# A gradient along rows: a strip of 512 columns of the last tile goes through DMAs of its own

## The chip, the cores and the metric

The kernel runs on one core of a Trainium2 chip. The metric is device time in microseconds (us): the time of one execution on the core, and over several runs the median. A profile of one execution, taken by the hardware profiler, goes with it; its span, from the first to the last instruction of the program, is a little shorter than the time of a run.

The engines that matter here are DVE (VectorE), POOL (GpSimd), SP (SyncE, which only issues DMAs here) and the core's 16 DMA engines, which move data between the chip's memory (HBM) and the core's memory (SBUF, 128 partitions).

## The reference

```python
def setup_inputs():
    return {
        "x": np.random.randn(8192, 8192).astype(np.float32),
    }

def reference(x: np.ndarray) -> np.ndarray:
    return np.gradient(x, axis=1)
```

Along each row, an inner element is `(x[j+1] - x[j-1]) / 2`; the first is `x[1] - x[0]` and the last `x[8191] - x[8190]`. All is float32. 268.4 MB are read and as many are written, and each row can be worked on by itself.

## The kernel before

**Tiles.** The 8192 rows are cut into `nsets` = 32 tiles of 256 rows. A tile lies in SBUF with two whole rows (`R` = 2) in each of the 128 partitions, so that a partition holds 65,536 B, in one piece in HBM as well. There are `NB` = 3 buffers (`slots`); tile i uses slot i % 3. A slot is 64 elements (`SH`) longer than a tile: the load writes from element 64 on, and the result is written from element 0 on, so it is made in place, running behind its input.

**One tile.** Six steps follow each other, each with the wait that it needs:

- L60, `load`: SP issues the load of the tile into its slot. From tile 3 on it waits for the store of the tile that had the slot before.
- L70: POOL computes the two end columns of each row (4 elements a partition) into `ends`, once the load has landed.
- L76: DVE computes all inner elements in one pass over 16,382 elements a partition, after L70. At the seam between the two rows and at their ends this pass leaves values that are no result.
- L87: the end columns are copied from `ends` over those places, by POOL for tiles with i % 5 of 1 or 3 (the last two excepted), else by DVE.
- L89: SP issues the store of the tile, after L87.
- After each third tile SP issues the next three loads.

**Order.** The program is in a fixed order (`tc.manual_schedule()`): each engine runs its instructions in the order in which the code names them. On SP that is load 0, 1, 2, store 0, 1, 2, load 3, 4, 5, store 3, 4, 5, and so on to load 30, load 31, store 30, store 31, since the last group has two tiles. All DMAs of the kernel stand in SP's one queue, and each tile DMA is spread over all 16 DMA engines: 128 pieces of 65,536 B, eight for each. POOL issues no DMA. `chain` keeps only the dependencies that it is given, and the order within a slot.

**What the change touches.** The loads at the start, `load` for the last tile, what follows tile 0 and tile 29 in the main loop, and the last store. In the order of SP, the new DMAs of the first half stand between load 0 and load 1 and between store 0 and store 1; on POOL the new DMAs of the second half stand between the end columns of tile 29 and those of tile 30; on DVE the new work stands behind L87 of tile 0 and behind L87 of tile 29.

Of the kernel before, what the change touches and what calls it, by code (L numbers as in the profile page):

```python
# [1 line left out]

# [4 lines left out]


@with_exitstack
def kernel(  # L10
    ctx: ExitStack,
    tc: tile.TileContext,
    x: bass.AP,
    out: bass.AP,
):

    nc = tc.nc
    P = nc.NUM_PARTITIONS
    n, m = x.shape
    R = 2
    NB = 3  # L30
    SH = 64
    W = R * m
    nsets = n // (P * R)
    f32 = x.dtype

    x_sets = x.rearrange("(s p t) m -> s p (t m)", p=P, t=R)
    out_sets = out.rearrange("(s p t) m -> s p (t m)", p=P, t=R)

    pool = ctx.enter_context(tc.tile_pool(name="pool", bufs=1))
    slots = [pool.tile([P, SH + W], f32, name=f"slot{k}", tag=f"slot{k}") for k in range(NB)]  # L40
    ends = pool.tile([P, nsets, R, 2], f32, name="ends", tag="ends")
    loads, stores = [], [None] * nsets
    in_front = {}

    def chain(i, ins, *needed):

        group, engine = f"slot{i % NB}", ins.ins.engine
        keep = [o.ins for o in needed]  # L50
        if in_front.get(engine, (None,))[0] == group:
            keep.append(in_front[engine][1])
        tc.declare_no_dep(ins.ins, group=group, keep=keep, reason="implied by the needed step")
        tc.add_to_no_dep_group(group, ins.ins)
        in_front[engine] = group, ins.ins
        return ins

    def load(i):
        b = slots[i % NB]
        ins = nc.sync.dma_start(out=b[:, SH : SH + W], in_=x_sets[i])  # L60
        loads.append(chain(i, ins, *([stores[i - NB]] if i >= NB else [])))

    with tc.manual_schedule():
        for i in range(NB):
            load(i)
        for i in range(nsets):
            b = slots[i % NB]
            xin = b[:, SH : SH + W].rearrange("p (t m) -> p t m", m=m)

            ins = nc.gpsimd.tensor_sub(  # L70
                out=ends[:, i, :, :],
                in0=xin[:, :, 1 : m : m - 2],
                in1=xin[:, :, 0 : m - 1 : m - 2],
            )
            at = [chain(i, ins, loads[i])]
            ins = nc.vector._custom_dve(  # L76
                dve_ops.TENSOR_TENSOR_REDUCE_SUB_MAX,
                out=b[:, 1 : W - 1],
                in0=b[:, SH + 2 : SH + W],
                in1=b[:, SH : SH + W - 2],  # L80
                s0=0.0,
                s1=0.5,
            )
            halved = chain(i, ins, *at)
            res = b[:, 0:W].rearrange("p (t m) -> p t m", m=m)
            placer = nc.gpsimd if i % 5 in (1, 3) and i < nsets - 2 else nc.vector
            ins = placer.tensor_copy(out=res[:, :, 0 : m : m - 1], in_=ends[:, i, :, :])  # L87
            placed = chain(i, ins, halved)
            ins = nc.sync.dma_start(out=out_sets[i], in_=b[:, 0:W])  # L89
            stores[i] = chain(i, ins, placed)  # L90
            if i % NB == NB - 1:
                for k in range(i + 1, min(i + 1 + NB, nsets)):
                    load(k)


# [1 line left out]
_INS = ['x']  # L97
_OUTS = [((8192, 8192), 'float32')]


# [23 lines left out]
```

## Time and profile before

| | |
|---|---|
| time, median of 3 runs | 1248.46 us (1248.35 to 1248.61) |
| span of the profiled execution | 1245.7 us |
| DVE's main pass (L76) | 32 x 17.22 us = 551.2 us |
| POOL waiting for loads to land (L70) | 989.6 us |
| data moved | 536.88 MB, 431 GB/s over the span |
| one tile load, from issue to landing (median) | 58.0 us |
| one tile store, from issue to landing (median) | 40.4 us |

The profiled execution is one execution; its own time isn't listed beside its span, and the median of the runs is 2.8 us above that span. Times inside the profile count from the start of the span. In the lines of the page, DMA digits are the busy share of the DMA engines in each of 40 slices, in tenths; `q1` is SP's DMA queue and `q14` the queue that brings instructions. In a timeline a line has the start, the duration, the engine, the source line and the operation, and in brackets the idle time before it with what ended it; `SPq` is the issue of a DMA by SP, and with `x2` it spans from the first issue to the end of the second.

### The profile page before, as it was taken

What the parts mean: (1) busy time and instruction counts of PE and PEld (TensorE: products, weight loads), DVE (VectorE), ACT (ScalarE), POOL (GpSimd) and SP (SyncE); (2) the same over time, 40 slices, a digit from 0 to 9 for tenths busy, and PEclk for the clock granted to TensorE, in tenths of its full rate; (3) what the DMA queues carried; (4) which work ended last, traced back from release to release, by engine and by line L of the source; (5) the groups of instructions that cost most, each with busy time, mean ns of one, the idle gap of its engine ahead of it and who ended that gap; (6) DMA issues with size and microseconds to landing.
All of it is one profiled execution on the core that took longest, in us unless ns stands there. A gap on an engine that the chain in (4) does not pass through costs nothing.

```text
span 1245.7 us, 237 instructions
## 1 busy us (share of the span) xinstructions
DVE 554.6 (45%) x52; POOL 8.8 (1%) x48
## 2 busy tenths in 40 slices
DVE  2850583069009702850582079009603840591083
POOL 0000000000000000000000000000000000000000
DMA  9999999999999999999999999999999999999999
GB/s 404 438 436 423 427 431 438 438 438 436 436 427 431 425 438 436 425 434 436 429 434 436 434 436 434 436 434 438 419 436 436 434 438 438 431 434 429 429 410 404
DMA packets 9217, 536.88 MB, mean 431 GB/s; under 512 B 1024, under 2 KB 1024, under 8 KB 1024
## 3 DMA queue, kind: packets, MB, share of 16 engines
q1 hardware_dynamic: 9216, 536.88, 99.8%
q14 instruction: 1, 0.01, 0.0%
HBM read 268.44 MB, written 268.44 MB: 431 GB/s over the span
## 4 chain that ended last, share of the span: by engine, by line
another core or an unknown queue 74%; DVE 18%; DMA 3%; issue 2%; POOL 1%; SPq 0%; POOLq 0%
DVE slot L76 18%; DMA slot<-in_x_dram 3%; POOL ends L70 0%; POOL slot L87 0%; SPq L60 0%; POOLq L119 0%; DVE slot L87 0%
## 5 line engine op out<-in xcount | busy, mean ns | idle before, releaser
L76 DVE CUSTOM_DVE_ANT_0 slot<-slot 128x16382 f32<-128x16382 f32 x32 | 551.2, 17224 | 668.7 <-POOL ends L70 668.7
L70 POOL TENSOR_TENSOR ends<-slot 128x4 f32<-128x4 f32 x32 | 6.3, 198 | 989.6 <-DMA slot<-in_x_dram 989.6
L87 POOL COPY slot<-ends 128x4 f32<-128x4 f32 x12 | 2.3, 190 | 207.9 <-DVE slot L76 207.9
L87 DVE COPY slot<-ends 128x4 f32<-128x4 f32 x20 | 3.4, 172 | 0.7
L108 POOL MEMSET const-bfloat16-1.0<- 128x1 bf16 x1 | 0.1, 101 | 0.0
L108 POOL MEMSET const-uint8-127<- 128x1 uint8 x1 | 0.1, 101 | 0.0
L108 POOL MEMSET const-float32-0.0<- 128x1 f32 x1 | 0.1, 98 | 0.2 <-issue 0.2
L108 POOL MEMSET const-float32-1.0<- 128x1 f32 x1 | 0.1, 98 | 0.0
## 6 DMA issues: line engine op xcount, KB each, us to landing
slot<-in_x_dram SPq DMA_DIRECT2D x32, 58.0
out_dram<-slot SPq DMA_DIRECT2D x32, 40.4
```

Of the source, the lines that this page charges most:

```text
L70: ins = nc.gpsimd.tensor_sub(out=ends[:, i, :, :], in0=xin[:, :, 1 : m : m - 2], in1=xin[:, :, 0 : m - 1 : m - 2],)
L76: ins = nc.vector._custom_dve(dve_ops.TENSOR_TENSOR_REDUCE_SUB_MAX, out=b[:, 1 : W - 1], in0=b[:, SH + 2 : SH + W], in1=b[:, SH : SH + W - 2],
L87: ins = placer.tensor_copy(out=res[:, :, 0 : m : m - 1], in_=ends[:, i, :, :])
L108: nc = _bacc.Bacc("TRN2", target_bir_lowering=False, num_devices=1)
```

## The change

The last tile (rows 7936 to 8191) is made 512 columns (`D`) narrower. Its load brings columns 0 to 7680 (one more than is stored, for the difference at the edge) and its store writes columns 0 to 7679, each as two pieces a partition instead of one. DVE's pass over the tile is not made shorter; what it computes to the right of the cut is not stored.

The 512 last columns of those 256 rows become two strips of 128 rows, in a new tile `strip` of 32 partitions with four rows each, for each half. Every strip DMA has eight rows of pieces (`G` = 8), one row of four in each of eight partitions, and four such DMAs carry a half.

- First half: SP issues its four loads behind load 0. After tile 0 DVE computes it (`strip_finish`: end column, difference, times 0.5, copy of the end column), and SP issues its four stores behind store 0.
- Second half: after tile 29, DVE clears a small tile `turn`; then POOL issues the four loads, each behind a small load of 8 x 64 B into `turn` (`other_engines`). DVE computes the half before it goes on to tile 30, and POOL issues the four stores, each again behind a small load into `turn`. The data in `turn` is used by nothing.

```diff
+    D = 512
+    G = 8
+    C = D + 1
+    last = nsets - 1
+    base = last * P * R
+
+    def tiles_of(dram):
+        return dram.rearrange("(s p t) m -> s p (t m)", p=P, t=R)
+
+    def cut_of(dram, width):
+        return dram.rearrange("(s p t) m -> s p t m", p=P, t=R)[last][:, :, 0:width]
+
+    def strip_of(dram, first, per, width):
+        rows = dram[base + first : base + first + G * per, m - width : m]
+        return rows.rearrange("(g q) w -> g q w", q=per)
+
+    x_sets, out_sets = tiles_of(x), tiles_of(out)
...
+    strip = pool.tile([P, 4, C], f32, name="strip", tag="strip")
+    tips = pool.tile([P, 4, 1], f32, name="tips", tag="tips")
+    turn = pool.tile([G, 8, 16], f32, name="turn", tag="turn")
+    queues = nc.sync, nc.gpsimd
...
     def load(i):
-        b = slots[i % NB]
-        ins = nc.sync.dma_start(out=b[:, SH : SH + W], in_=x_sets[i])
+        b = slots[i % NB][:, SH : SH + W]
+        of = x_sets[i]
+        if i == last:
+            b = b.rearrange("p (t m) -> p t m", m=m)[:, :, 0 : m - D + 1]
+            of = cut_of(x, m - D + 1)
+        ins = nc.sync.dma_start(out=b, in_=of)
         loads.append(chain(i, ins, *([stores[i - NB]] if i >= NB else [])))
 
+    def strip_part(dram, half, k, width):
+        rows = strip_of(dram, half * G * 16, 16, width)[:, 4 * k : 4 * k + 4, :]
+        first = half * P // 2 + k
+        return rows, strip[first : first + 4 * (G - 1) + 1 : 4, :, 0:width]
+
+    def other_engines(half, k):
+        if half:
+            nc.gpsimd.dma_start(out=turn[:, k, :], in_=x[0:G, 0:16])
+
+    def strip_loads(half):
+        for k in range(4):
+            rows, cells = strip_part(x, half, k, C)
+            other_engines(half, k)
+            queues[half].dma_start(out=cells, in_=rows)
+
+    def strip_finish(half):
+        part = slice(half * P // 2, half * P // 2 + 4 * G)
+        cells, tip = strip[part], tips[part]
+        inner = cells[:, :, 0 : C - 2]
+        nc.vector.tensor_sub(out=tip, in0=cells[:, :, C - 1 : C], in1=cells[:, :, C - 2 : C - 1])
+        nc.vector.tensor_sub(out=inner, in0=cells[:, :, 2:C], in1=inner)
+        nc.vector.tensor_scalar_mul(inner, inner, 0.5)
+        nc.vector.tensor_copy(out=cells[:, :, C - 2 : C - 1], in_=tip)
+        for k in range(4):
+            rows, cells = strip_part(out, half, k, D)
+            other_engines(half, 4 + k)
+            queues[half].dma_start(out=rows, in_=cells)
+
     with tc.manual_schedule():
-        for i in range(NB):
-            load(i)
+        load(0)
+        strip_loads(0)
+        load(1)
+        load(2)
         for i in range(nsets):
             b = slots[i % NB]
+            width = m - D if i == last else m
...
-            ins = nc.sync.dma_start(out=out_sets[i], in_=b[:, 0:W])
+            to, of = out_sets[i], b[:, 0:W]
+            if i == last:
+                to, of = cut_of(out, width), res[:, :, 0:width]
+            ins = nc.sync.dma_start(out=to, in_=of)
             stores[i] = chain(i, ins, placed)
+            if i == 0:
+                strip_finish(0)
+            if i == last - 2:
+                nc.vector.memset(turn, 0.0)
+                strip_loads(1)
+                strip_finish(1)
```

More of the change, by code (lines that the diff above doesn't have):

```diff
@@ L34 @@
     f32 = x.dtype
-    x_sets = x.rearrange("(s p t) m -> s p (t m)", p=P, t=R)
-    out_sets = out.rearrange("(s p t) m -> s p (t m)", p=P, t=R)
+    D = 512
[11 more added lines that the diff above has]
+    x_sets, out_sets = tiles_of(x), tiles_of(out)
     pool = ctx.enter_context(tc.tile_pool(name="pool", bufs=1))
```

## The prediction

> **What bounds the kernel now.** I read the busy shares and DMA queues first, then windows and the timeline at the end, then the DMA packet records.
>
> From the page (engines, slices, queues):
>
> ```profile
> span 1245.7 us, 237 instructions
> DVE 554.6 (45%) x52; POOL 8.8 (1%) x48
> ...
> DMA  9999999999999999999999999999999999999999
> ...
> q1 hardware_dynamic: 9216, 536.88, 99.8%
> q14 instruction: 1, 0.01, 0.0%
> ```
>
> The 16 DMA engines are full: SP's queue holds packets for 99.8% of 16 engines' span. The packet records say the same: each engine moves 512 packets of 65,536 B; the usual one takes 2.418 us, so 1238.0 us. The rest is 4.2 us in slower packets (mostly the first of a store after a load), 0.6 us in 4-byte completion packets (9 ns each), 1.7 us before the first packet and 1.2 us after the last: 1245.7 in all (neighbouring packets overlap by some 4 ns, 2 us an engine, about as much as the hole below). The change moves the same bytes, so the most that it could win is a few us.
>
> Windows (stretch, length, DVE, POOL, granted PE clock, DMA share, GB/s):
>
> ```profile
> 1128.00:1187.00 59.00, 0.00 (x0) 0.07 (x1) 1.00 1.01 438
> 1203.00:1205.50 2.50, 1.56 (x2) 0.00 (x0) 1.00 0.49 210
> 1205.50:1225.00 19.50, 17.40 (x2) 0.20 (x1) 1.00 1.05 454
> ```
>
> There is one hole: half the DMA time from 1203.0 to 1205.5. The timeline tells why:
>
> ```profile
> 1127.16 0.17 DVE L87 COPY slot<-ends 128x4 f32<-128x4 f32 x1
> 1127.36 0.33 SPq L89 DMA_DIRECT2D out_dram<-slot  x1
> 1128.95 19.64 SPq L60 DMA_DIRECT2D slot<-in_x_dram  x2
> 1186.93 0.20 POOL L70 TENSOR_TENSOR ends<-slot 128x4 f32<-128x4 f32 x1 [77.07 <-DMA slot<-in_x_dram]
> 1187.17 17.22 DVE L76 CUSTOM_DVE_ANT_0 slot<-slot 128x16382 f32<-128x16382 f32 x1 [59.84 <-POOL ends L70]
> 1204.42 0.17 DVE L87 COPY slot<-ends 128x4 f32<-128x4 f32 x1
> 1204.62 19.69 SPq L89 DMA_DIRECT2D out_dram<-slot  x2
> 1206.28 0.20 POOL L70 TENSOR_TENSOR ends<-slot 128x4 f32<-128x4 f32 x1 [19.14 <-DMA slot<-in_x_dram]
> 1206.51 17.23 DVE L76 CUSTOM_DVE_ANT_0 slot<-slot 128x16382 f32<-128x16382 f32 x1 [1.91 <-POOL ends L70]
> 1223.77 0.17 DVE L87 COPY slot<-ends 128x4 f32<-128x4 f32 x1
> ```
>
> Tile 30 lands at 1186.9. Its arithmetic and its store's start take 18.5 us (the store is issued at 1204.62, its first packets start at 1205.47). Meanwhile the load of tile 31 (8 x 2.418 = 19.3 us an engine) ends on the engines between 1202.8 and 1205.8, by following each engine's packets. So 15 engines wait 0.1 to 2.8 us (mean 1.6) and one, the slowest, does not. From there the two last stores run without a hole to 1244.5. The end is therefore set by: tile 30's landing on the slowest engine, 18.5 us, and two stores.
>
> **The change, part by part.**
>
> *Smaller last tile.* Per engine, eight packets of 2.418 us become sixteen half ones. By rate (65,536 B in 2.418 us, 27.1 B/ns) 30,720 B take 1.134 us, so 16 take 18.14 instead of 19.34, less 0.07 for eight more packets at 9 ns: 1.13 us less for the load and for the store. The store's 1.13 counts in full. The load's does not: the store of tile 30 waits for arithmetic, 18.5 us after tile 30's landing, and the shorter load (18.2) only makes the hole longer, on the slowest engine too. DVE works the full width as before; that chain stays.
>
> *SP's strips.* Four loads between the loads of tiles 0 and 1, four stores behind store 0: eight issues of 0.34 us, hidden behind 19.3 us packets already queued (without that cover 2.7 us). On eight engines each brings 16 pieces of 2,052 B in and 16 of 2,048 B out. A piece is 0.076 us by rate; the fixed part is between 9 ns (a completion packet) and 268 ns (the extra explained below), so 16 pieces cost 1.4 to 5.5 us. They stand in one ring with their neighbours, as the completion packets do: I take 1.4 in and 1.4 out.
>
> *Early DVE work.* Two passes over 4x511 elements at 1.051 ns (17,224 ns for 16,382) and two copies of 0.17: 4.65 us between tile 0 (done at 40.4) and tile 1 (landing at 42.0, with the strips 43.4). Tile 1 starts near 45.3, 3 us late, and its store, queued on SP behind the four strip stores, is issued near 62.8 instead of 59.8; it is needed when store 0 ends, at 81.8. Store 2 moves by less than 1 us. Cost nothing; without that cover 3 us.
>
> *Pool's strips.* The memset of `turn` follows tile 29's copy on DVE, so Pool issues four decoys and four loads from about 1127.5. A Pool issue isn't in this trace: between SP's 0.34 us and the 1.0 us from SP's first issue to its first packet; I take 0.7. Eight are 5.6 us in Pool's idle 77 us. SP's queue has stores 28 and 29 and loads 30 and 31 standing until 1205, so each Pool packet takes its turn. One row shows a turn: the instruction packet (8,192 B) at 997.7 us was served on one engine between the third and fourth 64 KB packets of one DMA, took 0.30 us, and the next packet took 2.686 instead of 2.418. So a turn comes after at most 2.42 us, and a foreign packet costs 0 to 0.27 us beyond its bytes. A strip DMA brings 4 pieces, 8,208 B, to an engine, about that packet's size: as one packet it costs 0.57 us and four cost 2.3. Completion packets and decoys (64 B an engine) lie between 9 ns and 0.27 us; four at the middle, 0.14, are 0.5 us. So loads add 2.8 us on the late eight engines. The early eight get four decoys at the full 0.27 (they change direction inside a store stream, where slow packets are found) and four completions, 1.6 us.
>
> *When they land.* Four to 24 turns (one for each DMA, or one for each piece, completion and decoy) are 10 to 58 us. I take 8, two a DMA, 19.4 us, since the 8 KB packet went in one: landed near 1149, DVE done near 1154, Pool's stores and decoys (4.9 us) issued by 1159 and through their 8 turns near 1179. Behind them on Pool stands tile 30's `ends` at 1186.9, and behind that DVE's main pass: 77 us of idle cover both; if it is gone each us late is a us at the end.
>
> On turns the row and the notes differ. The Trainium skill (DMA: Bandwidth & Descriptors, "Queues, rings and completion order") says that an engine drains a whole packet, typically 9 to 17 descriptors, before it turns to another queue. A turn would then be a whole tile DMA of 19.3 us, eight turns 155 us; the strips would land only as SP's queue runs dry near 1206, and DVE, Pool and two stores after that would end near 1281 in the median's terms. The packet served after three of eight speaks against it, and I go by the row.
>
> *The sum.* Before tile 30's landing the early eight gain 1.4 + 1.4 + 1.6, and 1.6 more for the store phase: 6.0 us. The late eight gain 2.8 + 2.8 = 5.6. Whichever half holds the slowest engine, the landing moves by 5.6 to 6.0, and I take 5.5, for the slow packets that overlap with it. Less 1.13 for the last store: +4.4 us. The profiled execution becomes 1250.1; the median of the runs stands 2.8 us above its span (1248.46 against 1245.7), which I keep: **1252.9 us**.
>
> Ends: by bytes alone, with Pool's stores in the hole, landing moves 1.2 to 2.4, so +0.1 to +1.3; with 268 ns a piece on SP's strips too, about +13.
>
> **The rivals.**
>
> *Strips cost only their bytes (not slower).* Place: the hole ahead of store 30. Price: if a foreign packet adds nothing (completion packets add 9 ns), the early eight gain 2.4 to 2.8 us and the late eight 1.2 to 1.4 each way, Pool's stores filling the hole. Landing moves 2.4, less 1.13: +1.3, 1249.8 us. It becomes a gain only from the point where the landing moves by less than 1.13, that is if the slowest engine is so far behind the eight that get most; the best is then -1.1, 1247.3. For it: completion packets cost 9 ns, and direction changes from store to load cost nothing in most groups. Against: the one foreign packet cost 0.57 us, not 0.30.
>
> *A new wait at tile 30.* If each piece takes a turn (24 x 2.42 = 58 us), strips land at 1186.5, DVE ends at 1191.2, Pool's seven issues at 1196.1, `ends` and the main pass at 1213.7, and store 30 starts at 1214.8 instead of 1205.5. +9.3 - 1.13 = +8.2: 1256.7 us; with issues of 1.0 us (+2.1) and two turns more (+4.8), 1263.6. It decides from 20 turns on: (1186.9 - 4.65 - 4.9 - 1128.4)/2.42. For it: the records show 64 KB pieces as packets of their own. Against: 8 KB went in one.
>
> *The change doesn't do what it says.* If the decoys don't steer, Pool's strips fall on the early eight: 2.8 + 2 x (2.3 + 0.5) = 8.4, less 1.13: +7.3, 1255.8 us. No row shows on which engines a Pool DMA of eight rows falls. The same page of the skill ("Why a DMA increments its semaphore by 16 and not by 1") says that it takes consecutive engines from a cursor that goes round, which the decoys rely on; no run here shows it.
>
> **How the numbers follow.** Forecast 0.45, bytes alone 0.34, new wait 0.14, no steering 0.07. About 0.2% (2.5 us) is what a measurement of this kernel tells from no change, so 1246.0 to 1251.0 is "same". Of bytes alone 0.03 is faster and 0.31 same; of the forecast, if foreign packets cost a third of the row, 0.05 is same. Faster 0.03, same 0.36, slower 0.61. The range cuts the gaining end of bytes alone (about 0.12) and the far end of the new wait (0.06): 1248.6 to 1262; the forecast's own range is 1250.5 to 1256.
>
> **What would show it.** Right: a DMA queue of Pool with strip packets spread over the stretch from 1128 on, 64 KB packets after them longer than 2.418 us; tile 30's `ends` some 5 us later than 1186.9; a longer hole ahead of store 30, about 1 us shorter from there to the end. Wrong: tile 30's `ends` waiting for POOL or DVE instead of the load (new wait); tile 30 landing at most 2.4 us later (bytes alone); eight engines far behind the other eight at the last load (no steering).

## The result and the profile after

Over 21 runs each on the same chips, the changed kernel takes 1249.48 us (1248.06 to 1251.13) and the kernel before 1248.10 us (1246.10 to 1248.91). The ratio is 1.0014, with a 95% interval of 1.0007 to 1.0020: 1.7 us (0.9 to 2.5) slower, which lies inside the 0.2% that the prediction calls "same". The profiled execution has a span of 1248.0 us against 1245.7: +2.3 us. The spans differ by more than the times: the runs whose spans are on record take 1.6 to 2.0 us longer than their span, and by that (an estimate) the profiled execution before lies some 0.5 us under its kernel's median, the one after 0.3 us over its own.

The page of the changed kernel (span, busy shares, DMA queues; `q0` is POOL's queue):

```profile
span 1248.0 us, 283 instructions
DVE 562.0 (45%) x61; POOL 18.5 (1%) x64
...
q1 hardware_dynamic: 9792, 536.35, 99.5%
q0 software_dynamic: 640, 0.53, 0.1%
```

The bytes are the same, the DMA engines are nearly as full as before, and 640 small packets have come in POOL's queue. The timeline of its end (start, duration, engine, line, operation; idle before and what ended it):

```profile
1129.43 0.17 DVE L138 MEMSET turn<- 8x128 f32 x1
1129.91 0.68 POOL L81 DMA_DIRECT2D turn<-in_x_dram  x1 [17.89 <-DVE turn L138]
1130.58 0.59 POOL L87 DMA_DIRECT2D strip<-in_x_dram  x1
...
1179.08 0.16 DVE L93 TENSOR_TENSOR tips<-strip 32x4 f32<-32x4 f32 x1 [49.48 <-DMA strip<-in_x_dram]
1179.16 2.27 DVE L94 TENSOR_TENSOR strip<-strip 32x2044 f32<-32x2044 f32 x1
1181.47 1.22 DVE L95 TENSOR_SCALAR strip<-strip 32x2044 f32<-32x2044 f32 x1
1182.61 0.16 DVE L96 COPY strip<-tips 32x4 f32<-32x4 f32 x1
...
1186.36 0.58 POOL L100 DMA_DIRECT2D out_dram<-strip  x1
1190.37 0.20 POOL L111 TENSOR_TENSOR ends<-slot 128x4 f32<-128x4 f32 x1 [3.43 <-DMA slot<-in_x_dram]
1190.60 17.22 DVE L117 CUSTOM_DVE_ANT_0 slot<-slot 128x16382 f32<-128x16382 f32 x1 [7.83 <-POOL ends L111]
1207.85 0.17 DVE L128 COPY slot<-ends 128x4 f32<-128x4 f32 x1
1208.05 19.28 SPq L133 DMA_DIRECT2D out_dram<-slot  x2
```

Three things are to be seen. Tile 30's `ends` start at 1190.37 instead of 1186.93, 3.44 us later. From there to store 30's issue it is 17.68 us, as before (17.69). From that issue to the end of the span it is 39.95 us instead of 41.05, 1.10 less. So 3.44 - 1.10 = 2.3 us: the whole change of the span is the later landing of tile 30 less the shorter last store. And POOL was done with the strip only 3.43 us before tile 30 landed: the new wait was nearly there.

The hole ahead of store 30 has grown, since the load of tile 31 is shorter and since the engines now end it further apart: by the packet records from 1203.2 to 1208.4 us, before from 1202.8 to 1205.8. Windows of the changed kernel (DVE, POOL, granted PE clock, DMA share, GB/s):

```profile
1203.00:1208.90 5.90, 4.99 (x2) 0.00 (x0) 1.00 0.37 158
```

63% of the DMA time in these 5.9 us stands empty, 3.7 us an engine, where before it was half of 2.5.

The durations of single DMA packets (medians) come from the packet records of the changed kernel:

```
SP's queue    2,052 B in    85 ns     2,048 B out   84 ns     30,724 B  1,139 ns    65,536 B  2,418 ns
POOL's queue  4,104 B (two pieces) 160 ns     4,096 B 159 ns     64 B 11 ns     8 B and 4 B  9 ns
```

### The profile page after: what moved, and what is told of

Read it like the earlier page. It is cut to its first block, busy times and chain, and to the rows that moved or that the text cites. A ratio compares the mean times of both kernels' runs of the same rounds, so it can differ in the third digit from the quotient of the medians.

```text
span 1248.0 us, 283 instructions
## 1 busy us (share of the span) xinstructions
DVE 562.0 (45%) x61; POOL 18.5 (1%) x64
## 4 chain that ended last, share of the span: by engine, by line
another core or an unknown queue 68%; DVE 21%; DMA 5%; issue 2%; POOL 1%; POOLq 0%; DVEq 0%
DVE slot L117 21%; DMA strip<-in_x_dram 4%; DMA slot<-in_x_dram 2%; POOL ends L111 0%; DVE strip L94 0%; POOL turn L81 0%; DVE strip L95 0%; POOL slot L128 0%; POOL out_dram L100 0%; POOL strip L87 0%; DVE slot L128 0%; DVE tips L93 0%; POOLq L169 0%; DVE strip L96 0%
## 5 line engine op out<-in xcount | busy, mean ns | idle before, releaser
L81 POOL DMA_DIRECT2D turn<-in_x_dram x8 | 4.5, 556 | 23.2 <-DVE turn L138 17.9
L94 DVE TENSOR_TENSOR strip<-strip 32x2044 f32<-32x2044 f32 x2 | 4.5, 2270 | 0.0
```

Source lines behind the costliest of these rows:

```text
L81: nc.gpsimd.dma_start(out=turn[:, k, :], in_=x[0:G, 0:16])
L94: nc.vector.tensor_sub(out=inner, in0=cells[:, :, 2:C], in1=inner)
```

## The experiments

Each was timed against the kernel before on the same chip; the times of both lie beside the ratio. "Landing" is the start of tile 30's `ends` in the profiled execution (before: 1186.93); in e5 that is not the end of the load. It is one execution each time: those of e3, e5, e7 and e10 are the shortest of theirs, 0.8 to 1.2 us under the median, and that of e8 lies 0.8 us over it.

| run | time, us | before, us | ratio (95%) | landing, us | span, us |
|---|---|---|---|---|---|
| changed kernel | 1249.48 | 1248.10 | 1.0014 (1.0007 to 1.0020) | 1190.37 | 1248.0 |
| e4 cut only | 1246.63 | 1247.82 | 0.9991 (0.9982 to 1.0000) | 1186.97 | 1244.5 |
| e3 SP's strip only | 1247.58 | 1247.82 | 1.0002 (0.9993 to 1.0010) | 1187.38 | 1245.0 |
| e2 POOL's strip only | 1247.79 | 1247.82 | 1.0000 (0.9991 to 1.0009) | 1187.60 | 1245.8 |
| e1 no decoys | 1249.81 | 1247.82 | 1.0019 (1.0010 to 1.0028) | 1189.87 | 1248.0 |
| e5 two decoys | 1260.93 | 1248.17 | 1.0105 (1.0091 to 1.0119) | 1200.64 | 1258.3 |
| e8 decoys alone | 1249.57 | 1248.17 | 1.0011 (1.0002 to 1.0020) | 1189.68 | 1248.5 |
| e6 SP on sixteen | 1249.86 | 1248.17 | 1.0014 (1.0005 to 1.0023) | 1189.69 | 1248.0 |
| e7 behind load 30 | 1248.38 | 1248.17 | 1.0001 (0.9992 to 1.0010) | 1186.21 | 1245.3 |
| e9 SP both halves | 1254.24 | 1248.12 | 1.0050 (1.0036 to 1.0063) | 1195.11 | 1252.6 |
| e10 steering decoys | 1248.80 | 1248.12 | 1.0007 (0.9999 to 1.0016) | 1188.63 | 1246.2 |
| e11 SP both, four DMAs | 1250.45 | 1248.50 | 1.0018 (1.0009 to 1.0027) | 1190.98 | 1248.8 |

### The parts one by one: e4, e3, e2

e4 keeps the cut and leaves both strips out:

```diff
         load(0)
-        strip_loads(0)
...
-            if i == 0:
-                strip_finish(0)
-            if i == last - 2:
-                nc.vector.memset(turn, 0.0)
-                strip_loads(1)
-                strip_finish(1)
```

> The last tile is cut, and neither strip is loaded, computed or stored (512 columns of 256 rows of the output are left out). Theory (the time is tile 30's landing, then a fixed chain and two stores): tile 30's ends stay at 1186.9 us within the 1 us by which executions differ, and from store 30's issue to the end it is 1.1 us shorter; span 1244.6, ratio to before 0.9991. Rival (the shorter load counts too, as bytes that no longer move): 2.3 us less, ratio 0.998.

It came out at 0.9991, and the landing stayed. Its timeline:

```profile
1186.97 0.20 POOL L108 TENSOR_TENSOR ends<-slot 128x4 f32<-128x4 f32 x1 [77.13 <-DMA slot<-in_x_dram]
...
1204.66 18.80 SPq L130 DMA_DIRECT2D out_dram<-slot  x2
1205.17 0.20 POOL L108 TENSOR_TENSOR ends<-slot 128x4 f32<-128x4 f32 x1 [18.00 <-DMA slot<-in_x_dram]
```

Tile 31 landed 1.11 us earlier than before (1205.17 against 1206.28), and nothing came of it: store 30 was issued 17.69 us after tile 30's `ends`, as always. Of two savings of 1.1 us, one is on the path.

e3 and e2 leave one half out each:

```diff
# e3: without the second half
-            if i == last - 2:
-                nc.vector.memset(turn, 0.0)
-                strip_loads(1)
-                strip_finish(1)
# e2: without the first half
-        strip_loads(0)
...
-            if i == 0:
-                strip_finish(0)
```

> SP's strip alone: the second 128 rows of 512 columns are left out, with Pool's DMAs and the decoys. Theory: sixteen pieces of 85 ns in and sixteen of 84 ns out lie on eight engines before tile 30's landing, so its ends start 2.7 us later than before (1189.6), less 1.1 at the last store: +1.6 us, ratio 1.0013. Rival (the cost is Pool's: switching between two queues): at most +0.3 us here, ratio 1.000.

> Pool's strip alone, with its decoys: the first 128 rows of 512 columns are left out. Theory: four packets of 160 ns and some twenty small ones of 9 to 11 ns an engine before tile 30's landing, +0.7 to 0.9 us (1187.7), less 1.1 at the last store: -0.3 us, ratio 0.9998. The forecast's price of a foreign packet (0.14 to 0.27 us beyond its bytes, some 20 of them before the landing): +3 to +5 us, less 1.1: ratio 1.002 to 1.003.

e2 is as the theory has it, and the forecast's price of a foreign packet is out: 1.0000, and from tile 29's `ends` to tile 30's it took 78.20 us instead of 77.26, +0.94. e3 is not: 1.0002 instead of 1.0013 (the interval ends at 1.0010), landing +0.45 instead of +2.7, in an execution 0.9 us under the median. Over e4, SP's strip costs 1.1 parts in a thousand, 1.4 us (the intervals leave about 1 us of doubt). Each half costs its share over e4 (1.1 and 0.9), and together with e4 they make 1.0011, the changed kernel within the intervals.

Where SP's other 1.3 us are is in the packet records. On each engine a DMA ends with a completion packet of 4 B; these are the starts, in us, of the sixteen that end load 29. Four executions without SP's strips and four with them:

```
                        SP's eight engines     the others
before                                         1106.2 to 1107.1 (10), 1107.8 (2), 1108.4, 1108.6, 1108.8, 1109.2
e4                                             1105.6 to 1106.9 (11), 1107.5, 1108.1, 1108.4, 1109.0, 1109.3
e2                                             1105.7 to 1107.2 (12), 1108.5, 1108.6, 1108.8, 1109.0
e7                                             1105.8 to 1107.9 (14), 1108.4, 1108.5
changed kernel          1109.6 to 1111.3       1106.5 to 1107.1
e3                      1108.1 to 1109.5       1105.6 to 1106.7
e1                      1109.2 to 1110.3       1107.5 to 1108.3
e5                      1109.6 to 1111.1       1106.8 to 1107.2
```

SP's eight get what the pieces last: when store 1 ends (near 103 us), the first DMA behind the strip's stores, they stand 2.6 to 2.9 us behind the others on average in these four runs, the 2.7 us of 16 x (85 + 84) ns. At load 29 it is 1.7 to 3.4 us. But a landing is made by the slowest of sixteen engines, and without strips some are by then 2 to 3 us behind the median. The slowest moves only from between 1108.5 and 1109.3 (without) to between 1109.5 and 1111.3 (with).

### Is it the slowest engine that counts? e6, e9, e11

e6 spreads SP's strip over all sixteen engines, by one DMA of 32 rows of pieces each way:

```diff
+    def whole(dram, width):
+        rows = dram[base : base + G * 16, m - width : m]
+        return rows.rearrange("(p q) w -> p q w", q=4), strip[0 : 4 * G, :, 0:width]
...
     def strip_loads(half):
+        if not half:
+            rows, cells = whole(x, C)
+            nc.sync.dma_start(out=cells, in_=rows)
+            return
```

> As the changed kernel, but SP's strip goes as one DMA of 32 rows of pieces over all sixteen engines: eight pieces in and eight out on each, 1.35 us instead of 2.7 on eight. Theory (the most loaded engine sets tile 30's landing): the landing is 1.35 us earlier than in the changed kernel, +2.1 over before, less 1.1: ratio to before 1.0005 to 1.0009. Rival (the mean over the engines counts): as the changed kernel, 1.0014.

1.0014 with an interval from 1.0005 to 1.0023: it can't tell the two apart. The landing (1189.69) is 0.7 us before the changed kernel's, and the slowest engine ends load 29 at 1111.0 instead of 1111.3. Two things work against spreading. Its pieces in took 126 ns on average instead of 85, so it costs 1.7 us an engine and not 1.35. And it burdens the engines that fall behind by themselves as well; that this weighs as much as it relieves is argued from e3, not shown.

e9 and e11 put both halves on SP's eight engines, early:

```diff
# e9
-    queues = nc.sync, nc.gpsimd
+    queues = nc.sync, nc.sync
...
         strip_loads(0)
+        strip_loads(1)
...
                 strip_finish(0)
+                strip_finish(1)
```

> Both halves of the strip by SP, early, on the same eight engines; Pool issues no DMA. Those eight get 32 small pieces in and 32 out before tile 30's landing, 5.4 us. Theory (only the slowest engine counts: the first 2.7 us on eight engines moved the landing by some 1.3, because other engines were behind anyway; from there on the eight are the slowest, and each further us counts): landing +1.3 + 2.7 = +4.0 us over before, less 1.1 at the end: +2.9 us, ratio 1.0020 to 1.0026. Rival (a small piece in SP's ring really costs half its 85 ns, since it overlaps with its neighbours): +1.3 + 1.3 - 1.1 = +1.5 us, ratio 1.0012.

1.0050, more than either theory: the edit brought a wait of its own. The timeline of e9 at its start, and two windows:

```profile
1.19 22.27 SPq L86 DMA_DIRECT2D strip<-in_x_dram  x8
...
23.50 0.91 SPq L70 DMA_DIRECT2D slot<-in_x_dram  x2
...
86.48 0.85 SPq L133 DMA_DIRECT2D out_dram<-slot  x2
```

```profile
20.00:26.00 6.00, 2.93 (x1) 0.20 (x1) 1.00 0.76 262
80.00:92.00 12.00, 4.02 (x2) 0.00 (x0) 1.00 0.75 317
```

SP issued the eighth strip load only when load 0 had landed (22.8 us), so load 1 was issued at 23.50 instead of about 5; the stores of tiles 1 and 2 slipped behind 86.48 in the same way. A quarter of the DMA time in both windows is empty. The trace names eight completion semaphores for SP's DMAs, and the ninth DMA waits for the first. e9 says nothing on the question.

e11 asks it again with four load and four store DMAs, as many as the changed kernel has:

```diff
-    D = 512
+    D = 448
...
+        rows = strip_of(dram, 0, 32, width)[:, 8 * k : 8 * k + 8, :]
+        return rows, strip[k : k + 4 * (G - 1) + 1 : 4, :, 0:width]
```

> As e9, but with four load and four store DMAs on SP's queue as the changed kernel has (eight rows of eight pieces each), and 448 columns instead of 512 so that it fits. The same eight engines get 32 pieces of 1,796 B in and 32 of 1,792 B out, 4.8 us, and the cut last store wins 1.0. Theory (only the slowest engine counts, and other engines were some 1.4 us behind anyway): tile 30's ends 3.4 us over before (near 1190.3), ratio 1.0017 to 1.0023; by the packet records the eight end load 29 some 4.8 us behind the other eight. Rival (a piece costs half its duration): the eight 2.4 us behind the others, landing +2.4 at most, ratio 1.0010 or less.

1.0018, landing +4.05. By the packet records the strip's eight stand 4.6 us behind the others at the end of store 1, near the 4.8 us that their 64 pieces last (75 and 74 ns), not half of it. At load 29 there are two groups of eight, from 1108.5 to 1109.5 and from 1112.3 to 1113.2, 3.8 us apart by their first. So pieces cost what they last, a first 2.7 us is partly taken up by engines that were behind anyway, and a second stands on the path.

### The foreign packets: e8, e1, e10

e8 is the kernel before with 112 decoys that nobody waits for:

```diff
+            if 2 <= i < nsets - 2:
+                for k in range(4):
+                    nc.gpsimd.dma_start(out=turn[:, 4 * (i - 2) + k, :], in_=x[0:8, 0:16])
```

> The kernel before, with 112 decoys of 8 x 64 B from Pool (four behind the end columns of each of tiles 2 to 29), which nothing waits for. Theory (a foreign packet costs its own 9 to 11 ns): 112 x 20 ns = 2.2 us on eight engines, 1.0 us on the others; +1 to +2.2 us, ratio 1.001 to 1.002. The forecast's price of 0.14 to 0.27 us for each of 224 packets: +31 to +60 us, ratio 1.025 to 1.05.

1.0011 (+1.4 us, 0.2 to 2.5), as by the packets' own 9 to 11 ns, which come to 2.1 us an engine. 3584 packets came in POOL's queue:

```profile
q1 hardware_dynamic: 9216, 536.88, 99.6%
q0 software_dynamic: 3584, 0.07, 0.2%
```

That is 224 an engine. The 64 KB packets right behind one of them took 2.431 us on average, the others 2.424 (median 2.418 for both), so the price of one beyond its own duration is some 7 ns at most. The 268 ns which the forecast took from the packet behind the one instruction packet do not show behind POOL's packets.

e1 takes the decoys out:

```diff
     def other_engines(half, k):
-        if half:
-            nc.gpsimd.dma_start(out=turn[:, k, :], in_=x[0:G, 0:16])
+        return
...
-                nc.vector.memset(turn, 0.0)
+                nc.vector.memset(strip[P // 2 :], 0.0)
```

> As the changed kernel, without the eight decoys (a memset of the second half's cells holds Pool until tile 29 instead). Theory: the four load DMAs carry their pieces alternately on the one eight engines and on the other, just as with decoys; 12 turns instead of 20, so the strips land some 17 us earlier (near 1163 instead of 1179); time down by 0.1 us at most, ratio to before 1.0013. If decoys steer: without them the placement of the pieces changes. If a foreign packet has a price of 0.14 us or more: at least 1 us faster than the changed kernel.

1.0019 (1.0010 to 1.0028): not faster than with decoys. The strips land at 1162.63 instead of 1179.08, and most of POOL's stores get in ahead of tile 30 (56 of 64 packets of 4,096 B):

```profile
1162.63 0.16 DVE L91 TENSOR_TENSOR tips<-strip 32x4 f32<-32x4 f32 x1 [31.87 <-DMA strip<-in_x_dram]
...
1166.61 2.15 POOL L98 DMA_DIRECT2D out_dram<-strip  x4 [33.21 <-DVE strip L94]
1189.87 0.19 POOL L109 TENSOR_TENSOR ends<-slot 128x4 f32<-128x4 f32 x1 [21.11 <-DMA slot<-in_x_dram]
```

From tile 29's `ends` (1110.86) it is 79.01 us, against 78.55 in the changed kernel, where 48 of those 64 packets come only behind tile 30's landing (and 16 of them after 1203, near the hole). The packets say that the decoys do nothing for the placement. What POOL's queue brought to one engine, in order, one packet between two 64 KB packets as a rule, in bytes:

```
changed kernel, one of SP's eight:  64 4 4104 4104 4   64 4 8 8 4         64 4 4104 4104 4   64 4 8 8 4
changed kernel, another engine:     4 4 8 8 4          4 4 4104 4104 4    4 4 8 8 4          4 4 4104 4104 4
e1, the one eight:                  4104 4104 4        8 8 4              4104 4104 4        8 8 4
e10, one of SP's eight:             256 4 8 8 4        256 4 8 8 4        256 4 8 8 4        256 4 8 8 4
e10, another engine:                16 4 4104 4104 4   16 4 4104 4104 4   16 4 4104 4104 4   16 4 4104 4104 4
```

With decoys or without, the strip's DMAs fall on the one eight and the other in turn, four 4,104 B packets on every engine; the decoys fall on SP's eight each time.

e10 gives the decoys the strip's form:

```diff
-            nc.gpsimd.dma_start(out=turn[:, k, :], in_=x[0:G, 0:16])
+            rows = x[0 : 4 * G, 0:16].rearrange("(g q) w -> g q w", q=4)
+            nc.gpsimd.dma_start(out=turn[0 : 4 * (G - 1) + 1 : 4, k, :, :], in_=rows)
```

> As the changed kernel, but each decoy has the strip's own form (eight rows of four pieces, each 64 B). Theory (a decoy of that form moves on the eight engines that the next Pool DMA gets, the plain decoy doesn't): all 64 load packets of the strip fall on one eight engines, eight each, and the decoys on the other. If that is the eight without SP's strips, tile 30's landing is set by SP's eight alone: about 1 us earlier than in the changed kernel (near 1189), ratio to before 1.0004 to 1.0009; if it is SP's own eight, 0.6 us later, ratio 1.0019. Rival (the form doesn't matter): four packets on each of the sixteen engines again, ratio 1.0014.

Now they steer: all 64 packets of 4,104 B fall on the engines without SP's strips. 1.0007 (0.9999 to 1.0016), landing 1188.63, 1.7 us before the changed kernel's, part of it because the execution that was profiled is a short one. From tile 29's `ends` (1110.97) to tile 30's it is 77.66 us, against 78.55 in the changed kernel and 77.26 before. The placement is shown; that it is worth 0.7 parts in a thousand (0.9 us) rests on this stretch and the ratio, as the intervals overlap. The Trainium skill (DMA: Bandwidth & Descriptors, "Why a DMA increments its semaphore by 16 and not by 1") has both: a Pool DMA takes consecutive engines from a cursor, and some direct copies are exempt and count as using all sixteen engines. The plain decoy, on SP's eight each time, fits the exemption, which the diff's scheme had not reckoned with; that it is this exemption is inferred.

### The wait that nearly came: e5

```diff
             other_engines(half, k)
+            other_engines(half, 8 + k)
             queues[half].dma_start(out=cells, in_=rows)
```

> A second decoy ahead of each of Pool's four strip loads: 28 turns instead of 20 up to the landing, 8 x 2.42 = 19.4 us more. Theory (a Pool packet waits for one 64 KB packet, and the changed kernel has only 3.4 us of cover left): the strips land near 1198, DVE is done near 1202, Pool has issued its stores near 1206.5, and only then come tile 30's ends, 16 us later than in the changed kernel; span near 1264, ratio to before 1.013 to 1.015. Rival (the landing is not set by turns, or has cover): ratio as the changed kernel, 1.0014.

1.0105, less than expected (1.013 to 1.015), for the strips land at 1192.55, 13.5 us later than in the changed kernel instead of 19.4. By the packet records the eight more turns were four 64 KB packets, three of load 31's of 30,724 B (1.14 us) and an SP completion packet of 9 ns, 13.1 us in all. The rest follows to the tenth:

```profile
1192.55 0.16 DVE L94 TENSOR_TENSOR tips<-strip 32x4 f32<-32x4 f32 x1 [63.13 <-DMA strip<-in_x_dram]
...
1200.03 0.59 POOL L101 DMA_DIRECT2D out_dram<-strip  x1
1200.64 0.21 POOL L112 TENSOR_TENSOR ends<-slot 128x4 f32<-128x4 f32 x1
...
1218.34 17.95 SPq L134 DMA_DIRECT2D out_dram<-slot  x2
```

Tile 30's `ends` have no wait for a load in front (its last engine was done at 1189.6): they stand right behind POOL's last store. 13.5 us less the cover of 3.4 are 10.1; `ends` start 10.3 us later, and the span is 10.3 us longer (1258.3 against 1248.0).

### The strip where the path is not: e7

e7 cuts the last tile in the same way and sends the whole strip through SP, behind load 30 and behind store 30:

```diff
+    def strip_load():
+        rows = x[base : base + P * R, m - C : m].rearrange("(p q) w -> p q w", q=R)
+        nc.sync.dma_start(out=strip, in_=rows)
...
                     load(k)
+                    if k == last - 1:
+                        strip_load()
...
+            if i == last - 1:
+                strip_finish()
```

> All 256 rows of the strip by SP over sixteen engines, loaded between the loads of tiles 30 and 31, computed on all 128 partitions behind tile 30 and stored between stores 30 and 31; Pool issues no DMA. Theory: tile 30's ends stay at 1186.9 us within 1 us; the strip's load (1.36 us) takes the place of the shorter load 31 (-1.13), and behind store 30 it is +1.34 - 1.13: +0.2 to +0.5 us, ratio 1.0002 to 1.0004. Rival (the bytes cost the same wherever they stand: 2.7 us in, 1.1 back): as the changed kernel, 1.0014.

1.0001 (0.9992 to 1.0010), landing 1186.21:

```profile
1186.21 0.20 POOL L89 TENSOR_TENSOR ends<-slot 128x4 f32<-128x4 f32 x1 [77.09 <-DMA slot<-in_x_dram]
...
1203.90 0.34 SPq L111 DMA_DIRECT2D out_dram<-slot  x1
```

The strip's load stands behind tile 30's landing and moves nothing: store 30 is issued 17.69 us after `ends`, as always. From there to the end it is 41.4 us instead of 41.05, for the strip's stores, 1.4 us an engine, take back the 1.1 that the cut saves. So over e4 all 256 rows in the same small pieces cost 1.0 part in a thousand, where in the changed kernel they cost 2.3. e7 ties with the kernel before and does not beat it.

## Why the prediction was right or wrong

- **The range held, the forecast was too high.** 1249.5 lies in 1248.6 to 1262, below the forecast's 1252.9 and its own range (from 1250.5). The nearest case was the rival that strips cost only their bytes (1249.8, chance 0.34). "Slower by over 0.2%" had 0.61; the change stayed inside 0.2%, which had 0.36. That the time lies in the range is owed to its lower end, which was drawn for that rival, and not to the forecast's sum.
- **What sets the end** was right: landing of tile 30 on the slowest engine, a fixed chain, two stores. After, e4, e5 and e7 all add up by it.
- **-1.13 for the last store, nothing for the load:** right, 1.10 in the profile and 0.9 parts in a thousand in e4.
- **SP's strips, 1.4 and 1.4:** the pieces cost that (85 and 84 ns), but as a term of the landing they were taken whole. The path got about 1.4 of 2.7, for the engines do not stand level.
- **The step that failed: a foreign packet's price beyond its bytes,** 0.27 for a decoy, 0.14 for a completion, 0.57 instead of 0.30 for a strip DMA. With it POOL's DMAs came to 3.2 us on SP's eight and, with their bytes, 5.6 on the others. Measured: 160 ns for two pieces, 9 to 11 ns for the rest, some 7 ns at most beyond (e8). The sign named for it, 64 KB packets longer than 2.418 us behind POOL's, did not come: their median stayed 2.418. POOL's half moved the landing by 0.9 us alone (e2) and 1.3 in the changed kernel (78.55 against 77.26 us from tile 29's `ends`).
- **The sum for the landing** was 5.5; it is 3.44: about 2.2 up to tile 29's `ends` (1111.82 against 1109.67) and 1.3 behind.
- **Turns:** that a foreign packet waits for one 64 KB packet, and not for a whole tile DMA, was right: from POOL's first packet to the last piece of its strip 16 of them passed on the later eight engines. Eight turns were wrong: some 20 passed (two beside SP's own completion packets), since pieces go in twos, and decoys, completions and DMAs without data on an engine take turns as well. The strips landed at 1179 instead of 1149. The rival's deciding point, landing by 1177.4, was passed; what kept it away is that issues (0.56 us instead of 0.7) and DVE's second pass (1.22 instead of 2.15) were cheaper and tile 30 itself landed 3.4 us later.
- **Early DVE work:** tile 1's store moved from 59.8 to 61.70 and nobody waited for it, as worked out.
- **The change does not do what it says:** that rival was half right. The decoys steer nothing; but the strips fall on all engines, not on SP's eight, which cost less than its 1255.8.

## What to carry to other kernels

Where DMA engines are full, ask first which transfer's landing starts the last chain: small pieces ahead of it cost their durations on the slowest engine, and behind it a load's pieces can be free (e7's were; its stores' were not). A transfer ends with its slowest engine, so an extra load on some engines is priced against how far the others lag, not whole. A DMA of a second queue costs little time beside a full one but waits a turn for each of its packets, and what waits for it should be given that long.

## What was not expected of the hardware

- **Engines drift apart.** In the kernel before, the sixteen engines end load 0 within 0.6 us of each other and load 29 within 3.1. Without strips they end load 29 over 2.7 to 3.7 us, with the last four or so behind; with SP's strips each group of eight is within 0.4 to 1.7 us. Why the spread within a group is smaller wasn't settled.
- **POOL held up by a DVE pass.** In the changed kernel POOL's `ends` of tile 1 took 0.81 us instead of 0.20, from 43.34 to 44.15, while DVE's scaling pass ran from 42.88 to 44.10:

```profile
42.88 1.22 DVE L95 TENSOR_SCALAR strip<-strip 32x2044 f32<-32x2044 f32 x1
43.34 0.81 POOL L111 TENSOR_TENSOR ends<-slot 128x4 f32<-128x4 f32 x1 [20.33 <-DMA slot<-in_x_dram]
```

This pass goes nearly twice as fast as the subtraction over as many elements (1.22 us against 2.27). In e11, with a longer pass, the same `ends` took 1.99 us. Nor is it the scaling pass alone. In e9 it was the subtraction, in e5 the main pass, with tile 31's `ends`:

```profile
44.30 2.27 DVE L93 TENSOR_TENSOR strip<-strip 32x2044 f32<-32x2044 f32 x1
45.78 0.85 POOL L111 TENSOR_TENSOR ends<-slot 128x4 f32<-128x4 f32 x1 [22.74 <-DMA slot<-in_x_dram]
```

```profile
1200.88 17.22 DVE L118 CUSTOM_DVE_ANT_0 slot<-slot 128x16382 f32<-128x16382 f32 x1 [4.66 <-POOL ends L112]
1208.97 9.19 POOL L112 TENSOR_TENSOR ends<-slot 128x4 f32<-128x4 f32 x1 [8.12 <-DMA slot<-in_x_dram]
```

Each time POOL's 0.2 us of work ended 0.05 to 0.07 us after DVE's pass. The Trainium skill (SBUF — State Buffer, "SBUF: two separate sides") says that GpSimd and a DVE instruction in a two-port mode, or one with two inputs in SBUF beside a GpSimd instruction that reads SBUF, lock each other out for a whole instruction; these rows agree.
